# Counting four tiles' top 256 as one group on VectorE, begun among the scores, with weight splits on GpSimd and pooled sums by halves, in a two-layer encoder on Trainium2

## The chip, the cores and the metric

The kernel runs on one core of one Trainium2 chip. Its time is the device time of one execution in microseconds (us), smaller being better; the time shown for a kernel is the median of its runs. The core's engines work side by side, each through its own instructions in order, and wait for each other by semaphores: TensorE (PE; PEld is its weight load), VectorE (DVE), ScalarE (ACT), GpSimd (POOL) and SyncE (SP), which here issues the DMAs.

## What is computed

Two layers of an encoder, for a prompt of 1024 rows and a sample of 32 rows with caches of 256 rows. Layer 0 has a convolution branch and attention with forget gates. Layer 1 has a pooling mixer over windows of 2, 4, 8 and 16 rows, and attention in which an indexer picks for each query the 256 keys of highest score. The change lies in layer 1, but for one buffer that both layers use. From the reference, cut to that:

```python
def multi_scale_pool(x, past, pos, w_grp, scale):
    xp = jnp.concatenate([past.astype(x.dtype), x], axis=1)
    ...
    for g, w in enumerate(POOL_WINDOWS):          # 2, 4, 8, 16
        ...
        outs.append((end[..., sl] - start) / cnt)  # mean of the last w rows
    pooled = (jnp.concatenate(outs, -1) - x.astype(jnp.float32)).reshape(B, T, N_POOL_GROUPS, POOL_GROUP)
    mixed = jnp.einsum('btgc,gcd->btgd', pooled, w_grp.astype(jnp.float32)).reshape(B, T, BRANCH)
    return (mixed * scale.astype(jnp.float32)).astype(x.dtype), xp[:, -POOL_PAST:]

def dsa_block(q, iq, iw, qpos, k, v, ik, kpos, topk):
    dots = jnp.einsum('bqhi,bsi->bqhs', iq.astype(jnp.float32), ik.astype(jnp.float32)) * IDX_DIM ** -0.5
    score = jnp.einsum('bqh,bqhs->bqs', iw.astype(jnp.float32) * IDX_HEADS ** -0.5, jax.nn.relu(dots))
    adm = (kpos[None, :] // CHUNK) <= (qpos // CHUNK)[:, None]
    score = jnp.where(adm[None], score, NEG)
    _, top_idx = lax.top_k(score, topk)
    ...
    s = jnp.einsum('bqhd,bqkhd->bhqk', q.astype(jnp.float32), k_sel.astype(jnp.float32)) * HEAD_DIM ** -0.5
    p = jax.nn.softmax(jnp.where(valid[:, None], s, NEG), axis=-1)
    return jnp.einsum('bhqk,bqkhd->bqhd', p, v_sel.astype(jnp.float32)).astype(q.dtype)
```

## The kernel before

**Projections.** Activations lie with channels on the partitions and tokens along the row, in four groups of 256 columns (the last has 288: the sample's 32 rows are appended). Each operand is split into a high and a low part, and a projection of 128 columns is 4 groups x 3 passes (high x high, low weight x high, high weight x low activation) x 8 matmuls (L208). A weight is fetched by a DMA (`wraw`), cast to its high part by ACT (`whi`, L106), and its low part is the difference (`wlo`, L107), computed by the engine in `low[0]`, in layer 1 VectorE; POOL computes 7 of the 62, all in layer 0. `proj_steps` prepares the next projection's weight at its fifth step (`ready`) and fetches the one after at its sixth.

**Work beside the projections.** After every pass of 8 matmuls `tick()` runs what was put off by so many ticks (`defer`), and steps the generators given to `background`. Each of these has a pace: the credit it gets per tick; what it yields is taken off that credit. The order on each engine is then set by the framework's scheduler, by when data are ready in its estimate, so instructions can stand in another order than in the code; `tc.keep_in_program_order` holds an instruction behind all that was traced before it on its engine.

**Layer 1, in order.** The indexer's projections with rope; the value projection with the scores (`scores`) beside it, seven tiles `sct` of 128 queries, widths 384, 512, 640, 768, 896, 1024 for tiles 0 to 5, and 288 for the sample (tile 6); then twelve projections in four groups c = 0 to 3, each of `c_val(c)`, `c_gate(c)` and `s_gate(c)`; then the first pair of heads' projection `qk1(0)` with the masks beside it; attention; the output layer.

**Top 256.** A tile's threshold is its 256th largest score, found bit by bit from the top: for each of 32 bits set the bit (`cand`), count the scores above, and keep the bit if the count stays high enough. `radix_v` does tiles 0, 1, 2 and 6 (`COL[:4]`) on DVE, as two groups of two: four counts per bit (L1243, on the upper halves `sch` for bits 31 to 16; `halve` then replaces these by the lower halves), and updates of `cond`, `thr`, `cand` (or `cond`, `tl`, `cl`) on 128x2. `radix_s` does tiles 3, 4 and 5 as a chain: ACT takes the sign of score minus candidate with the sum of the signs (`jka`, L1282), POOL updates the candidate (`gain`, `half` or `first`, `neg`, L1303 to L1309); 32 bits x 3 tiles = 96 signs. A clean-up on DVE for these tiles follows (L1311 to L1324).

**Pooling mixer.** `c_val(c)` copies each group's result to `cpad` (two buffers). `sums` builds the sum over 2, 4, 8 or 16 rows by doubling (`wb`, L1438, c + 1 ops), `pool_c` the mean minus the value (`pd`, L1444) and its two parts `plh`, `pll`, all per group of 256 columns, so four times per c. `mix` multiplies by the small matrix (PE, L1457), then by the scale and the gate (`sgm`, L1458), and splits the product (`cgh`, `cgl`).

**Masks.** `masking` goes over the tiles 0 to 6 in three steps: `s1` takes the sign against the threshold (`nd` on DVE, `sg` on ACT, `eq` on DVE), `s2` transposes `eq` on PE, `s3` counts ties by matmuls and writes the mask on DVE.

**Key rows out.** `k_out` (L292 to L304) transposes a pair of heads' keys on PE into a tile `ko` that a DMA writes out. In the half that holds the sample's rows, `kos` for these uses the same single buffer (tag "ko").

Of the kernel before, what the change touches and what calls it, by code (L numbers as in the profile page):

```python
# [32 lines left out]
def tile_encoder(ctx: ExitStack, tc, A, O):  # L33
# [258 lines left out]
    def k_out(l, p, hf, n, kf, pl):  # L292
        ps = ps_t()
        ko = pl.tile([128, 4, 128], FT, name="ko", tag="ko", bufs=1)
        for j in range(4):
            pe.transpose(ps[:, j * 128:(j + 1) * 128], kf[:, j * 128:(j + 1) * 128], ident)
        act.activation(ko, ps.rearrange("p (j c) -> p j c", j=4), AF.Copy)
        sp.dma_start(O["k_p"][l][hf * 512:(hf + 1) * 512, p * 128:(p + 1) * 128].rearrange("(j q) c -> q j c", q=128), ko)
        if n > 512:
            ps = ps_t()  # L300
            kos = pl.tile([DS, 128], FT, name="kos", tag="ko", bufs=1)
            pe.transpose(ps[:DS, :128], kf[:, 512:544], ident)
            act.activation(kos, ps[:DS, :128], AF.Copy)  # L303
            sp.dma_start(O["k_s"][l][:, p * 128:(p + 1) * 128], kos)  # L304
# [30 lines left out]
    PACE = (1.2, 0.5, 0.62)  # L335
# [688 lines left out]
    jkd = wt.bitcast(BF)  # L1024
    with tc.tile_pool(name="p4", bufs=1, reuse_waits="tile") as p4:
# [101 lines left out]
        def scores():  # L1127
            for i in range(6):
# [22 lines left out]
            defer(2, dve.tensor_copy, sch[6], top(sct[6]))  # L1151

# [29 lines left out]
    def radix_v():  # L1182


        def update(c0, c1, cnt, ks, b):

            cs = slice(c0, c1)
            if cnt is not None:
                dve.tensor_tensor(cond[:, cs], cnt, ks, op=OP.is_lt)
# [12 lines left out]
        def halve(c0, c1):


            cs = slice(c0, c1)
            dve.tensor_copy(sv[:, cs], thr.bitcast(U16).rearrange("p (n two) -> p n two", two=2)[:, cs, 1])
            dve.tensor_copy(hv[:, cs], thr.bitcast(BF).rearrange("p (n two) -> p n two", two=2)[:, cs, 1])
            dve.tensor_scalar(gv[:, cs], sv[:, cs], 32768.0, -2.0, op0=OP.is_ge, op1=OP.mult)
            dve.tensor_scalar(gv[:, cs], gv[:, cs], 1.0, None, op0=OP.add)
            dve.tensor_scalar(sv[:, cs], sv[:, cs], 32768.0, 65535.0, op0=OP.is_ge, op1=OP.mult)  # L1210
            for c in range(c0, c1):
                i = COL[c]
                n = SCW[i]
# [4 lines left out]
                dve.tensor_scalar(lw, low, gv[:, c:c + 1], sv[:, c:c + 1], op0=OP.mult, op1=OP.add)
                dve.scalar_tensor_tensor(sch[i].bitcast(U16), sch[i], hv[:, c:c + 1], lw, op0=OP.is_equal, op1=OP.mult)
                yield 0.3 + n * 0.0026  # L1220
            dve.tensor_tensor(ksl[:, cs], ksd[:, cs], cntd[:, cs], op=OP.subtract)
            dve.memset(tl[:, cs], 65535.0)
            dve.memset(cl[:, cs], 32767.0)

        def lower(c0, c1, b):
# [12 lines left out]
            yield

        def count(c, b, *ups):  # L1240
            n = SCW[COL[c]]
            x = sch[COL[c]]
            dve.tensor_scalar(jkd[:, :n], x if b > 15 else x.bitcast(U16), (cand[:, c:c + 1].bitcast(FT) if b > 15 else  # L1243
                              cl[:, c:c + 1]), None, op0=OP.is_gt, op1=OP.add, accum_out=cntd[:, c:c + 1])
# [82 lines left out]
    def masking(p4):  # L1327
# [11 lines left out]
        def s1(i):  # L1339
# [3 lines left out]
            sg = p4.tile([128, n], BF, name="sg", tag=f"sg{i % 3}", bufs=1)  # L1343
            eq = p4.tile([128, n], BF, name="eq", tag=f"eq{i % 3}", bufs=1)
# [7 lines left out]
        def s2(i):  # L1352
# [3 lines left out]
            eqT = p4.tile([128, nb, 128], BF, name="eqT", tag=f"eqT{i % 2}", bufs=1)  # L1356
# [33 lines left out]
        for i in range(9):  # L1390
            if i < 7:
                if i == min(COL[ND:]):
                    for _ in ra:
                        pass
                s1(i)
                yield 0.3 + SCW[i] * 0.0004
            if 0 < i < 8:
                s2(i - 1)
                yield 0.2
            if i > 1:  # L1400
                s3(i - 2)
                yield 0.3 + SCW[i - 2] * 0.002

    with tc.tile_pool(name="p4c", bufs=1, reuse_waits="tile", side="right") as p4:
# [5 lines left out]
        def c_val(c):  # L1410
# [4 lines left out]
            def ev_cv(g, t0, n, ps, cpad=cpad):  # L1415
                act.activation(cpad[:, 15 + t0:15 + t0 + 256], ps[:, :256], AF.Copy)
# [15 lines left out]
        def sums(c, g, cpad):  # L1432
            a, n = 256 * g, (271, 318)[g // 3]
            src, w = cpad[:, a:a + n], 1
            for lv in range(c + 1):
                dst = p4.tile([128, 318], FT, name=f"wb{lv % 2}", tag=f"wb{lv % 2}", bufs=2)
# [3 lines left out]
            defer((2, 2, 3, 4)[c], pool_c, c, g, cpad[:, a:a + n], src, w, n)  # L1440

        def pool_c(c, g, x, src, w, n):
            pd = p4.tile([128, 304], FT, name="pd", tag="pd", bufs=2)
            dve.scalar_tensor_tensor(pd[:, :n - 15], src[:, 15:n], 1.0 / w, x[:, 15:n], op0=OP.mult, op1=OP.subtract)  # L1444
            if g == 0:
                dve.tensor_tensor(src[:, 15:14 + w], src[:, 15:14 + w], rcn[:, 0:w - 1], op=OP.mult)
                dve.tensor_tensor(pd[:, :w - 1], src[:, 15:14 + w], x[:, 15:14 + w], op=OP.subtract)
            ph, pl = (p4.tile([128, 304], FR, name=nm, tag=nm, bufs=6) for nm in ("plh", "pll"))
            split(ph[:, :n - 15], pl[:, :n - 15], pd[:, :n - 15], alone=True)
            pooled[c, g] = ph, pl  # L1450

        def mix(c, g, n, pwh, pwl, sgc):
            px = ps_t()[:, :n]
            ph, pl = pooled.pop((c, g))
            for c0, at, m in ((0, 0, 256), (256, 271, DS))[:1 + g // 3]:
                for i, (a_, b_) in enumerate(((pwh, ph), (pwl, ph), (pwh, pl))):
                    pe.matmul(px[:, c0:c0 + m], a_, b_[:, at:at + m], start=i == 0, stop=i == 2)  # L1457
# [17 lines left out]
        rd, ra = radix_v(), radix_s()  # L1475
# [50 lines left out]
    sctx.close()  # L1526
    roles.update(ATT)
# [82 lines left out]
```

## Time and profile before

| | us |
|---|---|
| median of 3 runs (lowest, highest) | 1311.17 (1309.62, 1311.51) |
| the profiled execution | 1309.82 |
| its span | 1308.1 |
| busy in the span: PE, DVE, ACT, POOL | 1208.9, 991.4, 705.6, 269.8 |

The span runs from the first to the last instruction of the profiled execution. "Busy" sums the durations on an engine; an engine whose share is low over the span can still be full in one stage, so shares are to be read by stage. In rows of groups the columns are: line, engine, operation, output <- input, shapes, count | busy us, mean ns of one | idle time of the engine just before, and what ended it. In rows in order of time: start, duration, engine, line, operation, shapes, and in brackets the idle time before it and what ended it. The profile's stages of layer 1: indexer projections 640 to 671 us, scores and values to 748, the four groups c = 0 to 3 to 937, the masks with the first heads to 982, attention to about 1204, output layer to the end.

### The profile page before, as it was taken

How to read it: one execution, taken by the hardware profiler on the slowest of the kernel's cores; microseconds unless marked ns; L12 is line 12 of the kernel's file. 1: busy time of each engine (PE TensorE's matmuls, PEld its weight loads, DVE VectorE, ACT ScalarE, POOL GpSimd, SP SyncE). 2: the span in 40 equal slices, each digit the busy share in tenths (PEclk: the TensorE clock that was granted, in tenths of full speed). 3: DMA queues.
4: the chain of work that ended last, by engine and by line, in shares of the span. 5: the costliest groups of instructions: out<-in, count | busy, mean ns of one | idle time of the engine just before them, and what ended most of it. 6: DMA issues, size and time to landing. Idle time of an engine off the chain costs nothing. (4 is left out here: it accounts for less than half of the span.)

```text
span 1308.1 us, 25434 instructions
## 1 busy us (share of the span) xinstructions
PE 1208.9 (92%) x9353; PEld 1146.7 (88%) x9353; DVE 991.4 (76%) x2228; ACT 705.6 (54%) x1520; POOL 269.8 (21%) x597
## 2 busy tenths in 40 slices
PE   8999999999898989999999969589998999889997
PEld 6999999989787878999988959489988888869997
DVE  4699999367676777558757799995576988787477
ACT  5111242388777776221367858586357878775110
POOL 0000051004343443000121436373111111100000
PEclk9999999999899999999999989799999999999999
DMA  7113321335222283642333212132324223563512
GB/s 217 50 50 90 119 56 54 110 116 154 82 66 81 66 272 112 188 134 87 121 94 92 84 33 67 45 95 75 110 75 102 66 82 86 185 187 110 170 37 97
DMA packets 167673, 134.64 MB, mean 103 GB/s; under 512 B 37274, under 2 KB 154994, under 8 KB 167548
## 3 DMA queue, kind: packets, MB, share of 16 engines
q1 hardware_dynamic: 167548, 133.02, 34.2%
q8 instruction: 73, 1.20, 0.4%
q14 instruction: 52, 0.43, 0.1%
HBM read 85.09 MB, written 42.48 MB: 98 GB/s over the span
## 5 line engine op out<-in xcount | busy, mean ns | idle before, releaser
L865 DVE SCALAR_TENSOR_TENSOR acc<-apad,vT,acc 128x1086 f32<-128x1086 f32 x120 | 156.3, 1340 | 1.1
L107 DVE TENSOR_TENSOR ptl<-bank,pth 128x512 fp32r<-128x512 f32 (+1 forms) x160 | 99.5, 633 | 39.9 <-ACT pth L106 38.4
L208 PE MATMUL bank<-x1h,whi 128*128 128x256 f32 (+3 forms) x848 | 129.3, 292 | 0.4 <-ACT rpx L976 0.3
L208 PE MATMUL bank<-x1h,wlo 128*128 128x256 f32 (+3 forms) x848 | 128.9, 291 | 0.0
L208 PE MATMUL bank<-x1l,whi 128*128 128x256 f32 (+3 forms) x848 | 126.9, 288 | 0.0
L208 PEld LDWEIGHTS bank<-x1h,wlo 128*128 128x128 f32 (+1 forms) x848 | 116.1, 193 | 1.6 <-issue 0.4
L208 PEld LDWEIGHTS bank<-x1h,whi 128*128 128x128 f32 (+1 forms) x848 | 115.2, 192 | 2.5 <-ACT rpx L976 0.8
L420 PE MATMUL bank<-ident,s 128*128 128x128 f32 x576 | 96.2, 280 | 21.5 <-ACT kos L303 9.9
L208 PEld LDWEIGHTS bank<-x1l,whi 128*128 128x128 f32 (+1 forms) x848 | 113.9, 190 | 1.5 <-issue 0.4
L208 PE MATMUL bank<-x0h,wlo 128*128 128x256 f32 (+1 forms) x768 | 114.3, 291 | 0.0
L374 ACT ACTIVATE s<-s,mn 128x896 f32<-128x896 f32 (+7 forms) x128 | 98.9, 773 | 28.2 <-DVE mn L371 26.9
L208 PE MATMUL bank<-x0h,whi 128*128 128x256 f32 (+1 forms) x768 | 112.9, 287 | 1.0 <-ACT kr L805 1.0
L208 PE MATMUL bank<-x0l,whi 128*128 128x256 f32 (+1 forms) x768 | 110.7, 284 | 0.0
L1282 ACT ACTIVATE jka<-sc,neg 128x768 bf16<-128x768 f32 (+2 forms) x96 | 99.7, 1038 | 9.2 <-POOL neg L1309 4.4
L208 PEld LDWEIGHTS bank<-x0h,wlo 128*128 128x128 f32 x768 | 103.4, 193 | 0.9
L106 ACT ACTIVATE pth<-bank 128x512 fp32r<-128x512 f32 (+1 forms) x160 | 85.8, 549 | 32.8 <-PE bank L420 31.7
L208 PEld LDWEIGHTS bank<-x0h,whi 128*128 128x128 f32 x768 | 100.8, 189 | 2.8 <-ACT kr L805 1.3
L208 PEld LDWEIGHTS bank<-x0l,whi 128*128 128x128 f32 x768 | 100.1, 188 | 0.8
L395 PE MATMUL bank<-pth,v 128*128 128x256 f32 (+1 forms) x320 | 93.2, 308 | 4.8 <-ACT pth L106 4.7
L107 DVE TENSOR_TENSOR wlo<-wraw,whi 128x1024 fp32r<-128x1024 f32 (+2 forms) x55 | 66.5, 1208 | 40.2 <-ACT whi L106 40.0
L420 PEld LDWEIGHTS bank<-ident,s 128*128 128x128 f32 x576 | 67.1, 142 | 33.5 <-ACT kos L303 11.0
L106 ACT ACTIVATE whi<-wraw 128x1024 fp32r<-128x1024 f32 (+2 forms) x62 | 65.0, 1050 | 56.6 <-PE bank L208 35.3
(420 smaller groups left out, 2749.3 us busy)
## 6 DMA issues: line engine op xcount, KB each, us to landing
wraw<-in_o_w_in_dram SPq DMA_DIRECT2D x26, 512.0 KB, 4.0
wraw<-in_e_w_in_dram SPq DMA_DIRECT2D x24, 512.0 KB, 4.0
sgd<-sgc SPq DMA_DIRECT2D x32, 128.0 KB, 2.2
out_dram<-ko SPq DMA_DIRECT2D x16, 256.0 KB, 3.3
vf<-vd SPq DMA_DIRECT2D x16, 256.0 KB, 3.1
ckb<-ckd SPq DMA_DIRECT2D x8, 512.0 KB, 4.5
sg<-sgd SPq DMA_DIRECT2D x32, 128.0 KB, 2.8
wraw<-in_e_w_out_dram SPq DMA_DIRECT2D x8, 512.0 KB, 3.7
```

The source lines that it names most:

```text
L106: up = act.activation(hi, src, AF.Copy)
L107: eng.tensor_tensor(lo, src, hi.bitcast(FT), op=OP.subtract)
L208: pe.matmul(ps, w[:, k, :], x[g][:, k, :], start=i == 0, stop=i == 23)
L374: act.activation(s[:, :n], s[:, :n], AF.Exp, bias=mn[:, c:c + 1], scale=-1.0, accum_out=grp[p, i][0][:, j, e:e + 1])
L395: pe.matmul(po[:, j0 * 128:j0 * 128 + w], v2[e][:, k, :], src[:, b0:b0 + w], start=k == 0 and x == 0, stop=k == 2 * i + 1 and x == 1)
L420: pe.transpose(ps[:, c:c + 128], pt[j][:, k * 128:(k + 1) * 128], ident)
L865: dve.scalar_tensor_tensor(ac, apad[c][:, j:j + 1086], vT[:, c, j:j + 1], ac, op0=OP.mult, op1=OP.add)
L1282: act.activation(jka[:, :n], sct[COL[ND + j]], AF.Sign, bias=neg[:, j:j + 1].bitcast(FT), accum_out=cnta[:, j:j + 1])
```

## The change

1. `kos` is no tile of its own any more, but the first 128 columns of the key tile itself, whose keys have been transposed by then.
2. `radix_v` treats its four tiles as one group: a bit is four counts, then one update on 128x4. Each count is pinned by `keep_in_program_order`. It starts while the scores still run, three ticks after the score of tile 6, and gets its own paces.
3. The scores and the masks go through the tiles in the order of `COL` (0, 1, 2, 6, 3, 4, 5).
4. `low[0]` is POOL from the value projection until the scores' memory is given back, after the first heads' projection: 18 more splits there (25 in all), 33 on DVE instead of 51 with these shapes.
5. The pooled sums are built per half (512 columns; the second has 559 with the sample and its history) instead of per quarter: 20 `wb` ops instead of 40, and 8 of `pd`, `plh`, `pll` each instead of 16.
6. Behind the value projection only the scores are run to their end, not all background work.

```diff
@@ k_out
-            kos = pl.tile([DS, 128], FT, name="kos", tag="ko", bufs=1)
+            kos = kf[:DS, 0:128]
             pe.transpose(ps[:DS, :128], kf[:, 512:544], ident)
             act.activation(kos, ps[:DS, :128], AF.Copy)
             sp.dma_start(O["k_s"][l][:, p * 128:(p + 1) * 128], kos)
...
-    PACE = (1.2, 0.5, 0.62)
+    PACE = (1.3, 0.64, 0.55, 0.8)
...
-    GA, ND = 2, 4
+    ND = 4
@@ radix_v, moved ahead of the scores; update, halve and lower as before
         def count(c, b):
...
+            tc.keep_in_program_order(ins)
+            return 0.29 + n * 0.00104
...
+        for _ in update(0, ND, None, None, 31):
+            pass
+        for b in range(31, -1, -1):
+            for c in range(ND):
+                yield count(c, b)
+            for _ in lower(0, ND, b) if b < 16 else update(0, ND, cntd, ksd, b - 1):
+                pass
+            yield 0.5
+            if b == 16:
+                yield from halve(0, ND)
+
+    def when(flag, gen, pace):
+        while not flag:
+            yield pace
+        yield from gen
...
         def scores():
-            for i in range(6):
+            for i in COL:
+                if i == 6:
+                    yield from score_sample()
+                    continue
...
+            defer(3, begun.append, 1)
...
-        background((scores(), PACE[0]))
+        begun = []
+        rd, marks = when(begun, radix_v(), PACE[3]), scores()
+        low[0] = pool
+        background((marks, PACE[0]), (rd, PACE[3]))
         for c in range(4):
             proj_cm(w1, 2048 + c * 128, 128, X1, lambda g, t0, n, ps, c=c: ev_v(g, t0, n, ps, c))
-        drain()
+        for _ in marks:
+            pass
         flush()
...
@@ the old radix_v
-        for b in range(31, -1, -1):
-            yield from counts(0, GA, b, b2)
-            b1 = updates(0, GA, b)
-            yield from counts(GA, ND, b, b1)
-            b2 = updates(GA, ND, b)
...
@@ masking
-        for i in range(9):
-            if i < 7:
-                if i == min(COL[ND:]):
+        for x in range(9):
+            if x < 7:
+                if x == ND:
                     for _ in ra:
                         pass
-                s1(i)
-                yield 0.3 + SCW[i] * 0.0004
+                s1(COL[x])
+                yield 0.3 + SCW[COL[x]] * 0.0008
...
@@ c_val
-                defer(1, sums, c, g, cpad)
+                if g % 2:
+                    defer(1, sums, c, g // 2, cpad)
...
-        def sums(c, g, cpad):
-            a, n = 256 * g, (271, 318)[g // 3]
+        def sums(c, hf, cpad):
+            a, n = 512 * hf, (527, 574)[hf]
             src, w = cpad[:, a:a + n], 1
             for lv in range(c + 1):
-                dst = p4.tile([128, 318], FT, name=f"wb{lv % 2}", tag=f"wb{lv % 2}", bufs=2)
+                dst = p4.tile([128, 574], FT, name=f"wb{lv % 2}", tag=f"wb{lv % 2}", bufs=2)
...
-        rd, ra = radix_v(), radix_s()
+        ra = radix_s()
         background((rd, PACE[1]), (ra, PACE[2]))
...
     sctx.close()
+    low[0] = dve
```

Where instructions stand before and after. First DVE, at the first pooled sum of c = 2. Before (the first rows are the last updates of `radix_v`):

```order
L1227 TENSOR_TENSOR cond<-cntd,ksl 128x2
L1229 SCALAR_TENSOR_TENSOR tl<-cond,tl 128x2
L1236 TENSOR_SCALAR thr<-tl,gv,sv 128x1 x2
L107 TENSOR_TENSOR wlo<-wraw,whi 128x1024
L1438 TENSOR_TENSOR wb_10730<-cpad 128x270
L1438 TENSOR_TENSOR wb_10732<-wb_10730 128x268
L1438 TENSOR_TENSOR wb_10734<-wb_10732 128x264
L1444 SCALAR_TENSOR_TENSOR pd<-wb_10734,cpad 128x256
```

After, at the same place (`wt,cntd<-sch,cl` is a count on lower halves):

```order
L1075 TENSOR_SCALAR cl<-tl 128x4
L1437 TENSOR_TENSOR wb_10670<-cpad 128x526
L1437 TENSOR_TENSOR wb_10672<-wb_10670 128x524
L1437 TENSOR_TENSOR wb_10674<-wb_10672 128x520
L1085 TENSOR_SCALAR wt,cntd<-sch_8108,cl 128x384
L1443 SCALAR_TENSOR_TENSOR pd<-wb_10674,cpad 128x512
L1085 TENSOR_SCALAR wt,cntd<-sch_8109,cl 128x512
L1445 TENSOR_TENSOR wb_10674<-wb_10674,rcn 128x7
```

Before, all 128 counts stand ahead of this place: 44 ahead of the first `wb` of c = 0, 41 more before that of c = 1, and 43 more before this one. After, 31 stand ahead of the first `wb` of c = 0, then 26, 19 (with `halve`) and 26 up to that of c = 3, and 26 behind it. The weight's `wlo` is gone from DVE.

Second DVE, behind the last gate product of c = 3. Before:

```order
L1458 SCALAR_TENSOR_TENSOR sgm<-bank_11821,vT,sgm 128x288
L104 CAST cgh<-sgm 128x288
L107 TENSOR_TENSOR cgl<-sgm,cgh 128x288
L107 TENSOR_TENSOR wlo<-wraw,whi 128x1024
L1346 TENSOR_SCALAR nd<-thr 128x1 x3
L1348 TENSOR_SCALAR eq<-sg 128x384
L1349 TENSOR_SCALAR nd<-nd 128x1
```

After, the same product is followed by 11 counts with their updates, and then by these rows, the clean-up of tiles 3, 4 and 5 with the last threshold writes of `radix_v` among them, up to the first `nd` of the masks:

```order
L1315 TENSOR_SCALAR wt,cnta<-sc_8054,thr 128x768
L1071 SCALAR_TENSOR_TENSOR tl<-cond,tl 128x4
L1317 TENSOR_SCALAR wt<-sc_8054,thr 128x768
L1078 TENSOR_SCALAR thr<-tl,gv,sv 128x1 x4
L1318 ISA wt,cand<-wt,sc_8054 128x768
L1318 ISA cand 128x1
L1315 TENSOR_SCALAR wt,cnta<-sc_8055,thr 128x896
L1317 TENSOR_SCALAR wt<-sc_8055,thr 128x896
L1318 ISA wt,cand<-wt,sc_8055 128x896
L1318 ISA cand 128x1
L1315 TENSOR_SCALAR wt,cnta<-sc_8056,thr 128x1024
L1344 TENSOR_SCALAR nd<-thr 128x1 x3
```

The counts and the clean-up have moved from ahead of the gate products to between them and the masks.

Third POOL, at the end of the sign chain. Before (`neg<-first` ends the last update; the memsets belong to the masks):

```order
L1303 TENSOR_SCALAR gain<-cnta,down 128x1
L1304 TENSOR_SCALAR first<-first,gain 128x1
L1306 TENSOR_SCALAR neg<-first 128x1
L1331 MEMSET trib 128x640
L1334 MEMSET masks 128x384
```

After:

```order
L107 TENSOR_TENSOR wlo<-wraw,whi 128x1024
L1301 TENSOR_SCALAR gain<-cnta,down 128x1
L1302 TENSOR_SCALAR first<-first,gain 128x1
L1304 TENSOR_SCALAR neg<-first 128x1
L107 TENSOR_TENSOR wlo<-wraw,whi 128x1024 x3
L1329 MEMSET trib 128x640
L1332 MEMSET masks 128x384
```

Splits have come between the updates. From the fourth update to the 96th there are eleven of them, one per projection; the last of the twelve projections' splits stands behind the chain with two of the first heads.

More of the change, by code (lines that the diff above doesn't have):

```diff
@@ L1024, in tile_encoder, with radix_v, update, halve @@
     jkd = wt.bitcast(BF)
+    def radix_v():
+        def update(c0, c1, cnt, ks, b):
+            cs = slice(c0, c1)
+            if cnt is not None:
+                dve.tensor_tensor(cond[:, cs], cnt, ks, op=OP.is_lt)
+                yield
+                dve.copy_predicated(thr[:, cs], cond[:, cs], cand[:, cs])
+                yield
+            if b < 16:
+                return
+            bit = ci[:, b:b + 1].to_broadcast([128, c1 - c0])
+            if b == 31:
+                dve.tensor_copy(cand[:, cs], bit)
+            else:
+                dve.tensor_tensor(cand[:, cs], thr[:, cs], bit, op=OP.bitwise_xor)
+            yield
+        def halve(c0, c1):
+            cs = slice(c0, c1)
+            dve.tensor_copy(sv[:, cs], thr.bitcast(U16).rearrange("p (n two) -> p n two", two=2)[:, cs, 1])
+            dve.tensor_copy(hv[:, cs], thr.bitcast(BF).rearrange("p (n two) -> p n two", two=2)[:, cs, 1])
+            dve.tensor_scalar(gv[:, cs], sv[:, cs], 32768.0, -2.0, op0=OP.is_ge, op1=OP.mult)
+            dve.tensor_scalar(gv[:, cs], gv[:, cs], 1.0, None, op0=OP.add)
+            dve.tensor_scalar(sv[:, cs], sv[:, cs], 32768.0, 65535.0, op0=OP.is_ge, op1=OP.mult)
+            for c in range(c0, c1):
+                i = COL[c]
+                n = SCW[i]
+                dve.tensor_scalar(jkd[:, :n], sch[i], thr[:, c:c + 1].bitcast(FT), None, op0=OP.is_gt, op1=OP.add,
+                                  accum_out=cntd[:, c:c + 1])
+                low = sct[i].bitcast(U16).rearrange("p (n two) -> p n two", two=2)[:, :, 0]
+                lw = wt.bitcast(U16)[:, SEQ:SEQ + n]
+                dve.tensor_scalar(lw, low, gv[:, c:c + 1], sv[:, c:c + 1], op0=OP.mult, op1=OP.add)
+                dve.scalar_tensor_tensor(sch[i].bitcast(U16), sch[i], hv[:, c:c + 1], lw, op0=OP.is_equal, op1=OP.mult)
+                yield 0.3 + n * 0.0026
+            dve.tensor_tensor(ksl[:, cs], ksd[:, cs], cntd[:, cs], op=OP.subtract)
+            dve.memset(tl[:, cs], 65535.0)
+            dve.memset(cl[:, cs], 32767.0)
+        def lower(c0, c1, b):
+            cs = slice(c0, c1)
+            dve.tensor_tensor(cond[:, cs].bitcast(FT), cntd[:, cs], ksl[:, cs], op=OP.is_lt)
+            yield
+            dve.scalar_tensor_tensor(tl[:, cs], cond[:, cs].bitcast(FT), -float(2 ** b), tl[:, cs], op0=OP.mult,
+                                     op1=OP.add)
+            yield
+            if b:
+                dve.tensor_scalar(cl[:, cs], tl[:, cs], -float(2 ** (b - 1)), None, op0=OP.add)
+            else:
+                for c in range(c0, c1):
+                    dve.tensor_scalar(thr.bitcast(U16)[:, 2 * c:2 * c + 1], tl[:, c:c + 1], gv[:, c:c + 1], sv[:, c:c + 1],
+                                      op0=OP.mult, op1=OP.add)
+            yield
+        def count(c, b):
+            n = SCW[COL[c]]
+            x = sch[COL[c]]
+            ins = dve.tensor_scalar(jkd[:, :n], x if b > 15 else x.bitcast(U16),
+                                    (cand[:, c:c + 1].bitcast(FT) if b > 15 else cl[:, c:c + 1]), None, op0=OP.is_gt,
+                                    op1=OP.add, accum_out=cntd[:, c:c + 1])
+            tc.keep_in_program_order(ins)
[10 more added lines that the diff above has]
+                yield from halve(0, ND)
@@ L1355, in s2 @@
             eq = held[i][1]
-            eqT = p4.tile([128, nb, 128], BF, name="eqT", tag=f"eqT{i % 2}", bufs=1)
+            eqT = p4.tile([128, nb, 128], BF, name="eqT", tag=f"eqT{COL.index(i) % 2}", bufs=1)
             held[i] += (eqT,)
```

109 lines of the change are left out of this document (17 added, 92 removed).

## The prediction

> **What bounds the kernel now.** The page's busy shares are means over stages with different limits, so I read the busy time by stage first, with the cuts at the start of each pooling group. A row gives start:end, length, busy microseconds and count of PE, weight load, DVE, ACT and POOL, and the granted clock.
>
> ```profile
> core 0: us, PE busy (x) PEld busy (x) DVE busy (x) ACT busy (x) POOL busy (x), PEclk, DMA share, GB/s
> 747.00:805.00 58.00, 45.06 (x326) 44.30 (x325) 57.68 (x232) 38.21 (x77) 29.53 (x84) 0.85 0.21 61
> 805.00:863.00 58.00, 42.12 (x316) 41.12 (x315) 57.68 (x238) 37.61 (x76) 27.20 (x88) 0.85 0.18 50
> 863.00:901.00 38.00, 34.37 (x269) 33.98 (x268) 21.78 (x57) 34.87 (x72) 28.27 (x79) 0.96 0.32 93
> 901.00:937.00 36.00, 36.00 (x300) 35.96 (x299) 26.57 (x63) 7.31 (x17) 1.48 (x5) 1.00 0.32 92
> ```
>
> Four groups of three projections do the same matmul work. In c=0 and c=1 DVE is full (57.68 of 58), PE idles a quarter of the time, and its clock is granted at 0.85. In c=2 DVE has nothing left to count, ACT is at 92%; in c=3 PE is at 100%. The second view is that of the waits, over 671 to 985 us (waiter <- releaser: total, times, longest):
>
> ```profile
> ACT cpad L1413 <- DVE pd L1444: 29.5, 2, 15.7
> PE bank L1457 <- DVE plh L104: 14.5, 2, 9.0
> PE bank L1457 <- DVE sgm L1458: 14.3, 3, 9.5
> ```
>
> PE waits 28.8 us at the small pooling matmul, and ACT 29.5 us at the cpad of the next group, both for pooled work that stands behind counts on DVE. Each ACT wait also holds up the sign chain behind it. The third view, ACT in order of time, dates the groups by their first copy into cpad:
>
> ```profile
> 751.70 0.64 ACT L1416 ACTIVATE cpad<-bank 128x256 f32<-128x256 f32 x2
> 805.80 0.37 ACT L1416 ACTIVATE cpad<-bank 128x256 f32<-128x256 f32 x1
> 863.49 0.37 ACT L1416 ACTIVATE cpad<-bank 128x256 f32<-128x256 f32 x1
> 903.01 0.38 ACT L1416 ACTIVATE cpad<-bank 128x256 f32<-128x256 f32 x1 [1.25 <-PE bank L208]
> 937.09 0.41 ACT L321 ACTIVATE sgc<-bank 128x288 f32<-128x288 f32 x1 [2.77 <-PE bank L208]
> ```
>
> So c=0, c=1 and c=2 take 54.1, 57.7 and 39.5 us, 151.3 in all, and c=3 34.1 to its last gate copy. This is where the change can earn.
>
> **Counts and pooled sums on DVE.** The durations, for 746.7 to 900.4 us, then (the cond row) for the whole run:
>
> ```profile
> L1243 DVE TENSOR_SCALAR_CACHE_REDUCE wt<-sch,cl 128x384 bf16<-128x384 uint16 (+1 forms) x64 | 43.8, 684 | 0.4
> L1243 DVE DVE_READ_ACCUMULATOR wt<-sch,cl 128x1 f32 x64 | 5.3, 82 | 0.0
> L107 DVE TENSOR_TENSOR wlo<-wraw,whi 128x1024 fp32r<-128x1024 f32 x9 | 11.0, 1218 | 0.2 <-ACT whi L106 0.2
> L107 DVE TENSOR_TENSOR pll<-pd,plh 128x256 fp32r<-128x256 f32 (+1 forms) x12 | 5.1, 434 | 0.1
> L1458 DVE SCALAR_TENSOR_TENSOR sgm<-bank,vT,sgm 128x256 f32<-128x256 f32 (+1 forms) x12 | 5.8, 488 | 6.6 <-PE bank L1457 6.6
> L1189 DVE TENSOR_TENSOR cond<-cntd,ksd 128x2 int32<-128x2 f32 x32 | 5.1, 161 | 0.0
> ```
>
> The two split rows give a line: (1.218 - 0.434) / (1024 - about 264) = 1.03 ns per element, and 0.16 us fixed. A pooled op on a half costs one fixed part less than on two quarters: 20 + 3 x 8 = 44 ops fewer, 44 x 0.16 = 7 us. One group of four saves 96 updates of 0.16, 15 us of busy time. Nine splits leave DVE here: 11 us. None of it counts by itself: what counts is whether DVE still ends last. In the new order the counts per group are 26, 19 (with the halving), 26 and 26. For c=2: 26 x (0.684 + 0.082) = 20 us of counts, 6.5 x 3 x 0.16 = 3 of updates, 6 sums and two each of pd, plh and pll at up to 0.7 = 8, and gate work of 4 x (0.49 + 0.29 + 0.43) = 5: 36 us, less some 0.07 us of overlap at each of 80 instructions, so 30 to 31. For c=1 the halving (three passes over the four tiles, each some 0.68 long, 8 us) brings the same; c=0 less, c=3 about 33. All lie below the 39.5 us that c=2 took without counts on DVE. **I take it that c=0 and c=1 then run at c=2's pace.**
>
> **What is late next: the sign chain.** ACT had little spare time in c=2. Its rows and those of the updates on POOL, same window:
>
> ```profile
> L1282 ACT ACTIVATE jka<-sc,neg 128x1024 bf16<-128x1024 f32 (+2 forms) x82 | 85.2, 1039 | 7.9 <-POOL neg L1309 4.4
> L1282 ACT ACTIVATION_READ_ACCUMULATOR jka<-sc,neg 128x1 f32 x82 | 15.4, 188 | 0.0
> L106 ACT ACTIVATE whi<-wraw 128x1024 fp32r<-128x1024 f32 x8 | 8.4, 1051 | 0.0
> L1303 POOL TENSOR_SCALAR gain<-cnta,down 128x1 f32<-128x1 f32 x81 | 32.6, 403 | 22.2 <-ACT jka L1282 20.4 <-ACT cpad L1413 0.7
> L1304 POOL TENSOR_SCALAR first<-first,gain 128x1 f32<-128x1 f32 x47 | 14.5, 308 | 4.4
> L1309 POOL TENSOR_SCALAR neg<-first,down 128x1 uint16<-128x1 f32 x48 | 16.6, 346 | 4.2
> ```
>
> A sign with its read-out is 1.04 + 0.19 = 1.23 us. Of the 82 signs c=2 holds 26, c=0 and c=1 hold 28 each, and the new ACT order keeps that. So the three groups take 3 x 39.5 + 4 x 1.23 = 123.4 us: **27.9 us gained**.
>
> **The splits on GpSimd.** These are POOL's price for one (there was no sign chain beside it), and what it did to DVE:
>
> ```profile
> 364.82 2.40 POOL L107 TENSOR_TENSOR wlo<-wraw,whi 128x1024 fp32r<-128x1024 f32 x1 [1.48 <-ACT whi L106]
> 365.07 2.42 DVE L107 TENSOR_TENSOR spl<-op,sph 128x256 fp32r<-128x256 f32 x1 [0.62 <-ACT sph L106]
> 396.44 2.40 POOL L107 TENSOR_TENSOR wlo<-wraw,whi 128x1024 fp32r<-128x1024 f32 x1
> 397.16 0.48 DVE L371 CUSTOM_DVE_ANT_0 s<-bank,s,mn 128x256 f32<-128x256 f32 x1 [0.17 <-DVE mn L371]
> ```
>
> A split lies in front of sign updates. An update takes 0.40 + 0.31 + 0.35 = 1.06 us, and three tiles take turns, so a tile's next sign comes due two signs later, 2 x 1.23 = 2.46: slack 1.4. While ACT casts whi (1.05) it produces no sign, which makes 2.45 against 2.40. The split just fits if it starts when whi ends, and holds the chain if an update is queued behind it earlier. Bounds per split: 0 and 2.40 us; the nearest row is the slack, so I take 0.5. Nine splits stand among the 82 signs of c=0 to c=2: **4.5 us lost** (0 to 22). POOL would be busy some 85 (29.5 + 27.2 + 28.3) + 9 x 2.4 = 107 of 128 us: no bound, but no longer idle.
>
> The rows also show that a 256-wide subtraction with two operands in SBUF, elsewhere 0.43 us, took 2.42 beside the split and ended with it, while one that reads a PSUM bank took its usual 0.48. In the new kernel the updates, wb, pll and cgl are of the first kind, and there is one of them about every 3 us, so a split holds DVE for some 1.2 us on the average, at most 2.4. That takes back what moving it gave; with three splits a group DVE goes from 31 to 34 or 35 us. In c=3, where PE sets the 34.1 us, this is about even: **1 us lost** (-1 to 7).
>
> [...]
>
> **The key rows of the sample (kos).** Of layer 0 and of the whole run, waits, and one instance:
>
> ```profile
> ACT kos L303 <- DMA out_dram<-ko: 6.5, 2, 3.6
> PE bank L420 <- ACT kos L303: 7.9, 3, 4.0
> ACT kos L303 <- DMA out_dram<-ko: 8.7, 4, 3.6
> PE bank L420 <- ACT kos L303: 9.9, 4, 4.0
> ```
>
> kos shares one buffer with ko and waits for ko's transfer; ACT then holds up what PE transposes next. Written into the key tile it waits for nothing that isn't done: 7.9 us in layer 0 and 2.0 in layer 1 (9.9 - 7.9). I take 6.5 for the first (3 to 8; ACT's own wait is 6.5). In layer 1 the tile is the rope buffer with two copies, so a later rope copy now waits for kos's transfer; +1 (-2 to 2). **7.5 us gained.**
>
> **The earlier start and the tail.** The value stage gets a first 31 counts among the scores and ahead of the first sums (20 to 24 us, with updates), into DVE time that its second half has to spare in part (25.42 of 37 busy), but the scores' two-operand ops meet splits, and a split stands ahead of the rope shuffles: 1.5 lost (-1 to 3). At the other end the new order leaves 11 counts, their updates and the clean-up of the sign tiles (three ops on each of three tiles) behind the last gate product. Before, DVE idled here:
>
> ```profile
> 710.00:747.00 37.00, 36.81 (x273) 34.22 (x273) 25.42 (x75) 31.07 (x69) 13.39 (x50) 1.00 0.34 95
> 928.20 0.52 DVE L1458 SCALAR_TENSOR_TENSOR sgm<-bank,vT,sgm 128x288 f32<-128x288 f32 x1 [0.94 <-PE bank L1457]
> 938.48 1.23 DVE L107 TENSOR_TENSOR wlo<-wraw,whi 128x1024 fp32r<-128x1024 f32 x1 [8.93 <-ACT whi L106]
> 928.10:982.20 54.10, 51.26 (x429) 47.46 (x428) 34.58 (x81) 28.63 (x64) 9.21 (x16) 1.00 0.34 87
> L1317 DVE TENSOR_SCALAR_CACHE_REDUCE wt<-sc,thr 128x768 bf16<-128x768 f32 (+2 forms) x3 | 3.4, 1141 | 0.1
> L1319 DVE TENSOR_SCALAR wt<-sc,thr 128x768 f32<-128x768 f32 (+2 forms) x3 | 2.0, 682 | 0.0
> L1320 DVE CUSTOM_DVE_ANT_0 wt<-wt,sc 128x768 f32<-128x768 f32 (+2 forms) x3 | 3.3, 1086 | 0.0
> ```
>
> Added: 11 x 0.77 + 2 of updates + 8.7 = 19 us, less one split, against 8.9 + 10.6 of idle time (54.1 - 34.6 = 19.5 in all). It fits in sum, not in order: the first nd and eq, before at 11 us behind that gate product, come at 17 or 18, and with them the signs on ACT, the rope copy queued behind these signs, and the transposes of eq on PE. I take **4 us lost** (-1 to 9).
>
> **Sum.** -27.9 + 4.5 + 1 - 7.5 + 1.5 + 4 = -24.4. The profiled execution took 1309.82 us (span 1308.1), a little under the median of 1311.17: 1285.4, so 1285. Taking the good ends of chain, c=3, tail, kos: -27.9 - 1 - 1 - 10 - 1 = -41, 1269.
>
> **Rivals.** (a) *DVE still ends last*: a split blocks every DVE op beside it for the whole 2.4, counts too. A group then needs 31 to 33 + 7.2 = about 40 us of DVE and as much of ACT, and with both full some 43: the gain in c=0 to c=2 is 151.3 - 129 = 22 without the 4.5, and c=3 loses 6.6 instead of 1. 1309.8 - 22 + 6.6 - 7.5 + 5.5 = 1292. For it speaks 365.07, against it that counts never slowed beside POOL's one-column updates. [...] 0.17. (b) *The sign chain doesn't bind*: three groups at c=3's 34.1 us, 102.3, gain 49: 1309.8 - 49 + 1 - 7.5 + 5.5 = 1260. Against it: 26 signs and the rest of ACT's work filled 34.87 of 38 us. 0.07. (c) *Slower*: the split queues on POOL ahead of finished signs, and DVE's stream makes it take turns at twice its 2.4 us; each of nine then holds the chain for 4.8: 43 us. 1309.8 - 27.9 + 43 + 1 - 7.5 + 5.5 = 1324. It decides from 3.2 us per split, where 28.9 us are gone. Against it: both splits above took 2.40, the one beside a blocked DVE op too. 0.06. (d) *The spreading does not do it*: the counts are ahead of the pooled ops as before, DVE stays full in c=0 and c=1, and only its lighter work (some 16 us, given back in half to blocking) and kos remain: about 1299; with a worse tail no change. 0.08. My forecast keeps 0.62 (1269 to 1290).
>
> **Range and chances.** 1263 to 1301 takes in the forecast, (a), most of (d) and the good half of (b), and leaves out (c) and the ends, under 0.2. Faster by over 0.2% (2.6 us, about what a measurement of this kernel can tell): 0.90; within: 0.03; slower: 0.07.
>
> **What would show it.** In the profile after: PE's waits at the pooling matmul for plh and sgm and ACT's cpad wait gone; DVE at 75 to 90% in c=0 to c=2 with the clock near 1; the last sign near 870 instead of 900; three groups of 40 to 42 us; wlo rows on POOL of 2.4 with long DVE subtractions beside them; no wait for kos in layer 0; a wait of some us on PE for eq or rpx after the last gate. I am wrong if DVE is still full in c=0, if POOL's splits are longer or hold neg, or if the masks come more than 10 us late.

## The result and the profile after

The changed kernel takes 1287.72 us (median of 4 runs, 1286.16 to 1289.86), the kernel before 1311.10: ratio 0.9825, 95% interval 0.9808 to 0.9842. The forecast was 1285, with a range of 1263 to 1301. The profiled execution took 1286.16 us (span 1284.3).

That total hides terms that missed and cancelled. The table splits the spans of this and of the later runs at the start of four kinds of projection, by the first matmul of each in PE's order of time: the second indexer query projection, the first `c_val`, each next group, and `qk1(0)`. Each row is one profiled execution, and some lie off their kernel's median (e9: 1262.73 against 1268.10). The first column runs from 649.0 to 653.9 among the rows with the edit of kos, where little differs that early; so a difference of a few us between two rows is not settled by the table alone. One of e3's four executions, 1896.70 us at a granted clock of 0.556, was in a slow state, so e3's time below is the median of the other three.

| span, us | to the second iq | iq and values | c=0 | c=1 | c=2 | c=3 | masks to the end | all |
|---|---|---|---|---|---|---|---|---|
| before | 663.8 | 86.7 | 55.7 | 57.0 | 42.5 | 37.8 | 364.7 | 1308.1 |
| after | 650.8 | 95.5 | 37.1 | 43.0 | 44.1 | 36.8 | 377.0 | 1284.3 |
| e1, kos alone | 650.0 | 86.3 | 55.8 | 57.1 | 43.0 | 37.8 | 364.5 | 1294.4 |
| e2, POOL from c=0 on | 649.8 | 88.2 | 37.1 | 42.1 | 44.4 | 36.8 | 379.1 | 1277.5 |
| e3, no split on POOL | 651.7 | 88.2 | 36.7 | 38.8 | 43.6 | 36.8 | 373.5 | 1269.4 |
| e4, no pin | 649.4 | 111.5 | 62.5 | 47.8 | 43.5 | 43.9 | 365.2 | 1323.8 |
| e5, pin alone | 662.2 | 86.5 | 38.2 | 45.6 | 44.0 | 55.9 | 370.2 | 1302.7 |
| e6, quarters | 649.6 | 96.6 | 37.3 | 40.2 | 46.1 | 40.8 | 376.1 | 1286.7 |
| e7, late clean-up | 650.4 | 97.0 | 37.1 | 42.9 | 44.6 | 36.8 | 380.1 | 1288.8 |
| e8, denser counts | 653.9 | 99.7 | 36.7 | 44.3 | 43.2 | 38.4 | 363.9 | 1280.1 |
| e9, e3 with e8 | 649.0 | 92.1 | 36.7 | 41.5 | 40.7 | 37.6 | 363.4 | 1261.0 |
| e10, e3, denser later | 650.6 | 88.2 | 36.7 | 42.7 | 41.6 | 43.9 | 366.8 | 1270.5 |
| e11, e3, no early start | 651.4 | 86.9 | 36.7 | 40.6 | 40.3 | 36.8 | 397.6 | 1290.3 |

So after against before: 13.0 gained up to the indexer, 8.8 lost in the value stage, 31.0 gained in c=0 to c=2, 1.0 gained in c=3, 12.3 lost from the masks on. The busy times of c=0 to c=3 after, with the columns of the prediction's first view:

```profile
746.30:783.40 37.10, 37.10 (x308) 36.83 (x307) 33.26 (x91) 36.05 (x74) 31.23 (x82) 1.00 0.30 86
783.40:826.40 43.00, 39.39 (x308) 39.15 (x307) 39.72 (x103) 36.86 (x75) 37.34 (x92) 0.92 0.27 75
826.40:870.50 44.10, 39.69 (x307) 39.46 (x306) 35.90 (x97) 36.97 (x75) 36.84 (x90) 0.92 0.26 74
870.50:907.30 36.80, 36.80 (x308) 36.76 (x307) 34.80 (x93) 7.89 (x18) 9.16 (x11) 1.00 0.32 91
```

DVE is at 90% in c=0 where it was full, and PE is at 100% in c=0 and c=3. The waits of 747 to 868 us answer to the three rows shown before: none names pd or plh, and sgm keeps 0.2 us.

```profile
ACT jka L1280 <- POOL neg L1307: 8.9, 10, 2.5
PEld bank L1457 <- ACT pstS L1425: 8.4, 2, 4.6
PE bank L1457 <- ACT pstS L1425: 8.0, 2, 4.4
...
PEld bank L1457 <- DVE sgm L1458: 0.2, 1, 0.2
```

In their place ACT waits 8.9 us for the sign chain's updates on POOL, and PE 8.0 us for two small copies on ACT that stand behind such signs. These two waits, 3.61 and 4.41 us, are all of PE's idle time in c=1 and c=2 (43.00 - 39.39 and 44.10 - 39.69). The rest of what these groups take beyond c=0 is PE itself, busy 2.3 and 2.6 us longer at a granted clock of 0.92.

### The profile page after: what moved, and what is told of

Same layout as the page of the kernel before. It is cut to its first block, busy times and chain, and to the rows that moved or that the text cites. A ratio compares the mean times of both kernels' runs of the same rounds, so it can differ in the third digit from the quotient of the medians.

```text
span 1284.3 us, 25312 instructions
## 1 busy us (share of the span) xinstructions
PE 1203.3 (94%) x9353; PEld 1143.3 (89%) x9353; DVE 991.8 (77%) x2063; ACT 703.1 (55%) x1520; POOL 309.9 (24%) x615
## 4 chain that ended last, share of the span: by engine, by line
PE 64%; DVE 12%; ACT 11%; issue 5%; POOL 4%; DMA 3%; SPq 1%; DVEq 0%; POOLq 0%; ACTq 0%
PE bank L208 30%; PE bank L566 14%; PE bank L241 4%; PE bank L420 3%; PE bank L395 3%; PE bank L289 2%; ACT s L374 2%; PE bank L290 2%; ACT pth L106 2%; DVE wt L1085 1%; PE bank L224 1%; DVE ptl L107 1%; DMA rps<-rpx 1%; DVE s L371 1%; POOL wlo L107 1%
## 5 line engine op out<-in xcount | busy, mean ns | idle before, releaser
L374 ACT ACTIVATE s<-s,mn 128x896 f32<-128x896 f32 (+7 forms) x128 | 98.8, 773 | 30.4 <-DVE mn L371 29.7
L1280 ACT ACTIVATE jka<-sc,neg 128x768 bf16<-128x768 f32 (+2 forms) x96 | 99.7, 1038 | 16.7 <-POOL neg L1307 8.9
L395 PE MATMUL bank<-pth,v 128*128 128x256 f32 x320 | 92.5, 307 | 4.2 <-ACT pth L106 4.1
L107 POOL TENSOR_TENSOR wlo<-wraw,whi 128x1024 fp32r<-128x1024 f32 x25 | 60.6, 2425 | 147.0 <-ACT whi L106 147.0
```

What stands on the lines that cost most here:

```text
L107: eng.tensor_tensor(lo, src, hi.bitcast(FT), op=OP.subtract)
L374: act.activation(s[:, :n], s[:, :n], AF.Exp, bias=mn[:, c:c + 1], scale=-1.0, accum_out=grp[p, i][0][:, j, e:e + 1])
L395: pe.matmul(po[:, j0 * 128:j0 * 128 + w], v2[e][:, k, :], src[:, b0:b0 + w], start=k == 0 and x == 0, stop=k == 2 * i + 1 and x == 1)
L1280: act.activation(jka[:, :n], sct[COL[ND + j]], AF.Sign, bias=neg[:, j:j + 1].bitcast(FT), accum_out=cnta[:, j:j + 1])
```

## The experiments

**e1: kos alone.** The kernel before with

```diff
-            kos = pl.tile([DS, 128], FT, name="kos", tag="ko", bufs=1)
+            kos = kf[:DS, 0:128]
```

> The kernel before with the one edit of kos. In the changed kernel layer 0 ended 13.6 us earlier. If kos alone is the cause, layer 0 gains 13.6 here too and the rest stays: about 1311.1 - 13.6 = 1297.5. By the term of the prediction (6.5 in layer 0, 1 in layer 1): 1303.6. If the larger gain comes from another order of layer 0 in the changed kernel: 1303 or more.

1296.34 against 1311.02 (0.9885, 0.9857 to 0.9913): 13.8 us up to the indexer, nothing behind it. It is kos alone, at nearly twice the term of 7.5. The reason shows in PE's order of time, in the kernel before, at one of the two long waits (start, duration, instruction; the bracket is the idle time before it):

```profile
335.60 1.22 PE L208 MATMUL bank<-x0h,whi 128*128 128x288 f32 x8
...
341.69 1.12 PE L420 MATMUL bank<-ident,s 128*128 128x128 f32 x4 [3.95 <-ACT kos L303]
...
344.63 2.23 PE L208 MATMUL bank<-x0h,wlo 128*128 128x288 f32 x8
```

The same eight matmuls took 1.22 us ahead of the wait and 2.23 behind it. Over this stretch (327 to 349 before, 326.6 to 341.7 in e1) PE does the same work, 117 and 116 matmuls, in 17.76 and in 14.92 us, at a granted clock of 0.84 and 1.00. The window of the kernel before:

```profile
327.00:349.00 22.00, 17.76 (x117) 16.45 (x118) 13.73 (x35) 14.25 (x32) 9.18 (x13) 0.84 0.18 49
```

and of e1:

```profile
326.60:341.70 15.10, 14.92 (x116) 13.99 (x116) 12.95 (x35) 12.79 (x30) 9.06 (x13) 1.00 0.20 54
```

So a wait of 4.0 us cost 6.9 (22.0 - 15.1): the wait, and 2.8 us of slower matmuls. The second, of 3.4, cost 5.2 (11.8 us from 398.7 on, 6.6 in e1). In the kernel before and in the changed one, behind their first 250 us, PE has eleven waits of 2.5 us and more (3.36 to 9.49), and behind each of them matmuls run at about this rate; full rate is back 4 to 6 us behind the end of ten of them, 3.0 us behind that of the other. Shorter waits were followed by slow matmuls too: behind one of 2.88 us in e9, eight of these took 2.12. Others were not (last section).

**e2 and e3: where the splits on GpSimd pay or cost.** In e2 `low[0] = pool` stands behind the value stage, in e3 nowhere.

```diff
-        low[0] = pool
         background((marks, PACE[0]), (rd, PACE[3]))
...
         ra = radix_s()
+        low[0] = pool
```

> The changed kernel with POOL taking the splits only from the first pooling group on, so that the value stage's splits are DVE's again. If the split ahead of the rope product on POOL costs the value stage its 9 us, 6 to 9 of them come back and c=0 to c=3 stay: 1279 to 1282. If the counts or the other order of the scores cost them: 1286 to 1289.

> The changed kernel with all weight splits on DVE. [...] If DVE needs the relief, the four groups grow by 8 to 15 us (12 splits of 1.2): 1288 to 1295.

e2 took 1279.05 (0.9746, 0.9722 to 0.9771), e3 1272.84 (0.9697, 0.9668 to 0.9725), so both beat the change, e3 by 14.9 us; e2 lies in the first of its cases, e3 below what was expected of it. e2 gets back 7.3 of the 8.8 us of the value stage. The chain there, in the changed kernel, POOL, DVE, ACT, PE each in order of time:

```profile
658.13 2.45 POOL L107 TENSOR_TENSOR wlo<-wraw,whi 128x1024 fp32r<-128x1024 f32 x1 [6.66 <-ACT whi L106]
660.52 1.46 POOL L984 TENSOR_TENSOR rps<-rps,sinT 128x544 f32<-128x544 f32 x1
...
662.31 0.71 DVE L986 TENSOR_TENSOR rpx<-rpx,rps 128x544 f32<-128x544 f32 x1
...
663.06 0.63 ACT L281 ACTIVATE qiz<-rpx 64x512 fp32r<-64x512 f32 x1 [3.91 <-DVE rpx L986]
...
665.54 0.36 ACT L1246 ACTIVATE vr<-bank 128x256 f32<-128x256 f32 x1
...
665.95 0.69 PE L1252 MATMUL bank<-ident,vr 128*128 128x128 f32 x2 [5.07 <-ACT vr L1246]
```

POOL idles 6.66 us at the split until its `whi` is there, and the rope product behind it in the queue goes only then; ACT waits for the rope, the copy of the value rows stands behind that on ACT, and PE waits 5.07 us. In e2 PE has no wait above 1.2 us in this stage. So what is lost is not only the split's own 2.4 us, but the place in the queue.

From e2 to e3 c=1 gains another 3.3 us, c=0 to c=2 together 4.5, and the masks and all behind them 5.6, the cause of which stays open. The mechanism in c=1 of the changed kernel:

```profile
796.53 2.39 POOL L107 TENSOR_TENSOR wlo<-wraw,whi 128x1024 fp32r<-128x1024 f32 x1
798.91 0.48 POOL L1301 TENSOR_SCALAR gain<-cnta,down 128x1 f32<-128x1 f32 x1
...
800.53 0.94 ACT L1280 ACTIVATE jka<-sc,neg 128x768 bf16<-128x768 f32 x1 [2.44 <-POOL neg L1307]
...
801.88 0.25 ACT L1425 ACTIVATE pstS<-bank 15x128 f32<-15x128 f32 x1
...
802.18 0.58 PE L1457 MATMUL bank<-plh,pwh 128*128 128x256 f32 x1 [3.61 <-ACT pstS L1425]
...
802.99 2.12 PE L208 MATMUL bank<-x1h,whi 128*128 128x288 f32 x8
804.91 2.12 PE L208 MATMUL bank<-x1h,wlo 128*128 128x288 f32 x8
```

One split holds a sign for 2.44 us, the sign holds the copy that PE waits for, PE waits 3.61 us and then runs at about half rate (2.12 us for eight matmuls that take 1.22 at full rate). The same group in e3, with the columns of the prediction's first view, has PE at a clock of 1.00:

```profile
776.70:815.50 38.80, 37.03 (x307) 36.79 (x307) 34.39 (x99) 35.30 (x72) 33.10 (x88) 1.00 0.29 80
```

The splits are not the only thing that delays this copy: in c=2 of e3 PE still waits 3.9 us for it (4.4 in the changed kernel), and in c=1 of e9, also without a split on POOL, 2.9 us. DVE did not miss the relief either: with all splits back its share in each of c=0 to c=3 stays below 96% (in all 140.15 of 156.0 us in e3, 143.68 of 161.0 after), since some of DVE's own work took longer beside a split on POOL. Of the changed kernel, DVE beside the split of 796.53, and beside one of 781.50 to 783.90:

```profile
796.45 0.87 DVE L1085 TENSOR_SCALAR_CACHE_REDUCE wt<-sch,cand 128x640 bf16<-128x640 bf16 x1
...
797.24 1.98 DVE L104 CAST plh<-pd 128x559 fp32r<-128x559 f32 x1
...
781.59 0.88 DVE L1085 TENSOR_SCALAR_CACHE_REDUCE wt<-sch,cand 128x640 bf16<-128x640 bf16 x1
...
782.52 0.51 DVE L1085 TENSOR_SCALAR_CACHE_REDUCE wt<-sch,cand 128x288 bf16<-128x288 bf16 x1
...
783.07 0.85 DVE L1031 TENSOR_TENSOR cond<-cntd,ksd 128x4 int32<-128x4 f32 x1
```

The counts run through at their usual 0.88 and 0.51. The small compare took 0.85 us (elsewhere 0.16) and ended when the split ended, the cast 1.98 (elsewhere 0.44), and it ended 0.3 us behind the split. What sets the counts apart is not shown.

**e4 and e5: the pin.** e4 takes `tc.keep_in_program_order` out of the changed kernel; e5 puts nothing but it into the kernel before.

```diff
@@ e4, against the changed kernel
-            tc.keep_in_program_order(ins)
@@ e5, against the kernel before
-            dve.tensor_scalar(jkd[:, :n], x if b > 15 else x.bitcast(U16), (cand[:, c:c + 1].bitcast(FT) if b > 15 else
+            ins = dve.tensor_scalar(jkd[:, :n], x if b > 15 else x.bitcast(U16), (cand[:, c:c + 1].bitcast(FT) if b > 15 else
                               cl[:, c:c + 1]), None, op0=OP.is_gt, op1=OP.add, accum_out=cntd[:, c:c + 1])
+            tc.keep_in_program_order(ins)
```

> The changed kernel without the pin on the counts; the counts then stand ahead of the pooled sums again (76 before the first). If the spreading is what gains in c=0 to c=2, PE's waits for plh and sgm return and most of the 31 us are lost: 1302 to 1315. If the lighter DVE work is what gains, the time stays within 4 us of 1287.7.

> The kernel before with nothing but each count pinned in order: two groups of two, quarters, splits on DVE. If order alone gains, c=0 to c=2 lose 20 to 30 us of their 151, less what moves to the tail: 1284 to 1293. If the lighter work is needed as well, DVE (137 us of work in these 151) still ends last and less than 12 us are gained: 1299 or more.

e4 took 1325.93 us, slower than before (1.0103, 1.0072 to 1.0133), and beyond what was expected: the early counts then push ahead of the scores as well (43 counts instead of 14 stand ahead of the last score operation, and the value stage takes 111.5 us), and c=0 to c=2 take 153.8, nearly as before. Among its waits, 649 to 915 us, are the old ones, for cpad, plh and sgm, and one of 14.5 us that ended with an update of the counts, cond:

```profile
PE bank L1456 <- DVE cond L1069: 14.5, 1, 14.5
...
PE bank L1456 <- DVE plh L104: 8.9, 1, 8.9
PE bank L1456 <- DVE sgm L1457: 4.7, 2, 3.8
...
ACT cpad L1410 <- DVE pd L1442: 27.9, 2, 20.0
```

e5 took 1303.36 against 1309.21 (0.9952, 0.9929 to 0.9974). The pin alone brings 27.4 of the 31.0 us in c=0 to c=2, as the first case has it. But 18.1 are given back in c=3 and 5.5 behind it, so the time falls into the second case, whose reason did not hold: neither expectation held for the whole. DVE is busy 51.69 of the 55.9 us of c=3:

```profile
876.60:932.50 55.90, 41.55 (x317) 40.66 (x316) 51.69 (x183) 11.47 (x27) 3.65 (x12) 0.88 0.24 69
```

**e11: the early start.** e3 with the counts begun only behind the value stage:

```diff
-        background((marks, PACE[0]), (rd, PACE[3]))
+        background((marks, PACE[0]))
```

> e3 (all splits on DVE) with the counts begun only behind the value stage: 4 instead of 31 ahead of the first pooled sum, so some 27 counts more in c=0 to the masks, 27 x 0.77 = 21 us of DVE. If the early start is what makes pinned counts fit, c=3 and the masks give back 10 to 20 us: 1283 to 1293. If DVE's lighter updates alone make them fit: 1270 to 1277, as e3.

1294.63 us (0.9897, 0.9871 to 0.9923), 21.8 more than e3, somewhat above the expected range. The groups don't grow; the last column, with the masks, does, by 24.1 us: the last count starts at 949.4 us instead of 896.0. Pinned work that is not done early is done at the end.

**e6: quarters.** The changed kernel with `sums`, `pool_c` and `mix` as before the change.

> The changed kernel with the pooled sums per quarter again (44 DVE ops more, about 7 us of DVE). If DVE ends last in c=1 (93% busy there), 2 to 5 us are lost: 1290 to 1293. If the sign chain ends last: within 1.5 us of 1287.7.

1289.41 us (0.9863, 0.9831 to 0.9894), 1.7 more than the change, between the two cases; the intervals overlap, so halves against quarters stays open. Within the span c=2 and c=3 take 6.0 us more and c=1 2.8 less.

**e7 and e8: the masks.** e7 holds the clean-up of the sign tiles behind the first four tiles' nd; e8 makes the counts denser.

```diff
@@ e7
+    late = []
     def radix_s():
...
-        dve.tensor_scalar(thr[:, ND:].bitcast(FT), neg.bitcast(FT), -1.0, None, op0=OP.mult)
+        while not late:
+            yield 1
+        tc.keep_in_program_order(dve.tensor_scalar(thr[:, ND:].bitcast(FT), neg.bitcast(FT), -1.0, None, op0=OP.mult))
...
                 if x == ND:
+                    late.append(1)
@@ e8
-    PACE = (1.3, 0.64, 0.55, 0.8)
+    PACE = (1.3, 0.72, 0.55, 1.2)
```

> The changed kernel with the clean-up of the sign tiles held behind the first four tiles' nd. If PE's 9 us stall at the transposes of eq comes from the counts and the clean-up ahead of nd, nd comes some 7 us earlier and 5 to 8 us are gained: 1280 to 1283. If something else (rope, the sign on ACT) ends last there: 1286 to 1289.

> The changed kernel with the counts paced faster (0.72 for 0.64, and 1.2 for 0.8 in the value stage), so that counts and clean-up are done within c=3. If the tail's stall is theirs, all of its 9 to 12 us go and c=0 to c=2 pay 2 to 6 for the denser counts: 1279 to 1284. If DVE then ends last in the groups, they pay 10 or more and the time is 1287 or above.

In the changed kernel nd came 19 us behind the last gate product, and PE waited for it:

```profile
898.10 0.51 DVE L1458 SCALAR_TENSOR_TENSOR sgm<-bank,vT,sgm 128x288 f32<-128x288 f32 x1
...
917.25 0.27 DVE L1344 TENSOR_SCALAR nd<-thr 128x1 f32<-128x1 f32 x3
...
918.50 0.50 PE L1361 MATMUL bank<-identb,eq 128*128 128x128 bf16 x3 [9.12 <-DVE nd L1347]
918.75 2.06 PE L208 MATMUL bank<-x1l,whi 128*128 128x256 f32 x8
```

e7 fits neither case: 1292.17 us (0.9885, 0.9855 to 0.9914), 4.5 more than the change, although nd comes 6.4 us earlier behind the gate product and PE's wait for it falls from 9.1 to 2.8 us. In its place PE waits for the rope's copy on ACT:

```profile
PE bank L208 <- ACT rpx L976: 6.5, 1, 6.5
```

Moving 9 us of DVE work within the stage only moves the wait. e8 takes it out of the stage: 1279.35 us (0.9784, 0.9755 to 0.9813), the masks and all behind them 13.1 us shorter, no wait of PE above 1.4 us there. The denser counts cost 4.2 in the value stage and 1.6 in c=3; c=0 to c=2, which were expected to pay 2 to 6, take the same 124.2 us.

**e9 and e10: the two put together.** e3 with e8's paces, and e3 with (1.3, 0.8, 0.55, 0.8).

> All splits on DVE, and the counts paced as in e8 (0.72; 1.2 in the value stage). If the two losses are separate, the gains add: e3's nine projections (119 us) and e8's tail (9 to 13 us shorter), less e8's 4 us in the value stage: 1262 to 1268. If DVE, with splits and denser counts, ends last in the groups, they grow to 125 or more: 1270 to 1276.

> All splits on DVE, the counts paced 0.8 in the groups and 0.8 in the value stage as in the changed kernel: the value stage keeps e3's 88 us, and counts and clean-up end within c=3. If the two losses are separate: 1258 to 1264, better than e9 by the value stage's 4 us. If the groups can't take the counts: 1267 to 1275.

e9 took 1268.10 (0.9658, 0.9623 to 0.9693), e10 1274.63 (0.9718, 0.9687 to 0.9749). e9 is the fastest of all and beats both kernels, the change by 19.6 us; it came out at the upper end of the first of its cases, its profiled execution at 1262.73. Its interval overlaps e3's, so the paces' share is not settled; by stage, the masks are 10.1 us shorter than in e3 and the value stage 3.9 longer, as separate losses would have it. e10 is the second of its cases: c=1 and c=3 grow by 3.9 and 7.1, and the masks gain 6.7.

## Why the prediction came out

**The main term's reason held, its size did not.** c=0 to c=2 were to gain 27.9 less 4.5 for the splits, 23.4, and gained 31.0 (29.7 by the prediction's own cuts, 151.3 to 121.6) with 4.5 to 5.1 lost to the splits (c=0 to c=2 take 124.2 after, 123.6 in e2, 119.1 in e3). DVE ceased to end last; e5, with the pin alone, and e4, without it, show that the order does most of it. That c=0 and c=1 take c=2's pace was the step that missed: c=2 before held a PE wait of 3.46 us itself. c=0 then ran at PE's own pace, 37.1 us with PE full (and ACT busy 36.05 us of them), while c=1 and c=2 took 43 and 44, the difference being one PE wait each and the slower matmuls behind it. So the sign chain was no floor under all three groups; it cost where one copy stood behind a sign, and rival (b) was right for one group of three.

**The sum was right because misses cancelled.** In the prediction's terms, besides these 31.0 for 23.4: kos was put at 7.5 and is worth 13.7 (e1); the value stage at 1.5 lost and cost 8.8; the tail at 4 and cost 12.3; c=3 at 1 lost and gained 1.0. kos, the value stage and the tail lie outside the bounds given for them. That the sum of 24.4 lies beside the measured 23.8 us of span is luck. kos, the value stage and the tail have one step in common that failed: a wait of PE was priced at its own length, or less where later work could catch up. The runs showed that PE runs the matmuls behind a wait of 3 to 9 us at about half rate (2.23 us for eight instead of 1.22, 17.76 against 14.92 for a stretch). With 9.12 us of waiting and slower matmuls behind it the tail comes near its 12, and e8, without that wait, has them back; the place of nd itself, 19.2 us behind the gate product, was nearly the 17 or 18 forecast. kos's two long waits of 4.0 and 3.4 came to 6.9 and 5.2.

In the value stage a second step failed, the reading of the split's place: the prediction had the split ahead of the rope product but charged nothing like the 6.66 us that POOL idles there for `whi`, with the rope behind it. The 1.5 us themselves are what the stage loses in e2 and e3, which have the counts there but not these splits (88.2 against 86.7).

**Splits on GpSimd.** Their price in c=0 to c=2, 4.5, came out at 4.5 to 5.1, but not as 0.5 at each of nine: 4.2 of the 5.1 us between the change and e3 fall in c=1, on one wait of PE and its slower matmuls. The forecast priced them as a small loss, 5.5 us with c=3; without them 14.9 us more are gained, most of that in the value stage and c=1. The blocking of DVE was foreseen at 1.2 us a split and showed, at about 1.3 (15.4 us more than usual for the operations beside the twelve splits of the four groups): cond took 0.69 on average (x9) against 0.16, and the pd of 559 columns 1.29 (x4) against about 0.74.

**Rivals.** (a), that splits also block counts, fell: counts ran at their usual 0.88 beside a split. (c), more than 3.2 us per split on the sign chain, fell: no wait of a sign was longer than 2.5 us, and c=0 to c=2 lost about 5 in all. (d), that the counts don't spread, is what e4 is, and it was worse than the price given (1326 against 1299), since the early counts then displace the scores too.

**What was not separated.** The one group of four (half as many updates) was not undone by itself, nor was the other order of the scores and masks, and halves against quarters lie within their intervals. The early start, which the prediction priced only as a loss, is worth 21.8 us in e11.

## What to carry to other kernels

Price a wait of TensorE with the slower matmuls that can follow it (here a wait of 4.0 us came to 6.9), and count such waits: the kernel before has seven of 2.5 us and more behind its first 250 us, the changed one four, e9 two. Spread filler work so that no consumer stands behind a run of it, but look where the rest of it lands: pinned work must start early enough to be finished where it hides. Before handing work to an idle engine, look at what stands behind it in that engine's queue; a 2.4 us instruction in the wrong place cost 7 us, and the engine it relieved did not need it.

## What the hardware showed that was not expected

TensorE's rate fell to about half behind a wait of 2.88 us (2.12 us for eight matmuls of 288 columns, 1.22 at full rate) as behind one of 9.12 (2.06 for eight of 256, 1.10 at full rate). It came back 4 to 6 us after the end of most waits (in c=1 of the changed kernel by 808.2, behind a wait that ended at 802.18), 3.0 us after the wait that ended at 842.46 in the kernel before, and in one case of e9, behind 2.87 us, 2.4 us after it. Among the shorter waits the length alone does not decide: behind 2.03 us in e11 the next eight matmuls take 2.12 us, behind 2.64 us in e6 they take 1.22. What does decide there stays open. PE in e9, e11 and e6, each in order of time:

```profile
795.89 0.38 PE L1456 MATMUL bank<-plh,pwh 128*128 128x256 f32 x1 [2.88 <-ACT pstS L1424]
...
797.73 2.12 PE L208 MATMUL bank<-x1h,wlo 128*128 128x288 f32 x8
...
792.23 0.38 PE L1456 MATMUL bank<-plh,pwh 128*128 128x256 f32 x1 [2.03 <-ACT pstS L1424]
...
792.84 2.12 PE L208 MATMUL bank<-x1h,whi 128*128 128x288 f32 x8
...
801.33 0.39 PE L1455 MATMUL bank<-plh,pwh 128*128 128x256 f32 x1 [2.64 <-ACT pstS L1424]
...
801.79 1.22 PE L208 MATMUL bank<-x1h,whi 128*128 128x288 f32 x8
```

In the changed kernel VectorE's small ops of 0.16 us on four columns took up to 2.39 us beside a GpSimd split, while its counts, with one input and an accumulator, stayed at or below 0.88 us, beside a split or not.
